# Two memory pairs worked in steps inside two stick-breaking pairs, with output and latent weights in other buffers

## The chip, the cores and the metric

The kernel runs on one core of one Trainium2 chip. The metric is the device time of one execution in microseconds (us). The core has five engines that work on queues of their own: TensorE (PE; its weight loads are shown as PEld), VectorE (DVE), ScalarE (ACT), GpSimd (POOL) and SyncE (SP), which here issues all DMA transfers.

## The reference

Two layers over 2048 tokens of width 1024. Each layer projects the normalized tokens once, and four groups of four heads (64 wide) use the result:

```
h = layer_norm(x); mem_n = layer_norm(mem)              # mem: 256 rows
for l in range(2):
    fq, fk, fv, f, sq, sk, sv, c_q, c_kv, k_rot, mq, gate = split(h @ w_in[l])
    fox: causal softmax(q k / 8 + cum(log_sigmoid(f + b))_q - cum(...)_k) v
    sb : w = sigmoid(z) * prod of (1 - sigmoid(z)) over the later valid keys;  w v   # z = q k / 8
    mla: q, k, v from rms_norm(c_q), rms_norm(c_kv) by two more weights; rope on 32 columns; causal softmax
    mem: softmax(mq mk / 8) mv     # mk, mv = mem_n @ w_mem_kv[l]; all 256 rows, no mask
    y = (concat(fox, sb, mla, mem) * silu(gate)) @ w_out[l]
    h = layer_norm(sqrt(2) * h + y)
```

## The kernel before

**Tiling.** Every factor of a matmul is held as two f16 parts (high and low), and a product is three matmuls (`mm3`, lines 276 to 278). Tokens are worked in 4 chunks of 512. The heads of a group are worked two at a time: a *pair* `fox0` is the first two heads of fox, and so on; eight pairs and one latent step (`lat`: c_q, c_kv, k_rot and the forget column for all tokens) make a layer. `PLAN` (line 45) is their order: lat, fox0, fox1, mla0, mla1, sb0, sb1, and at the end mem0 and mem1 side by side. After them comes the output projection with the layer's normalization (`out_proj`).

**A pair** is a generator (line 707). Its first step loads and splits four weights (`wprep`: load, absolute maximum, a scale by `allmax`, high part on ACT at L146, low part on the DVE at L147). Then each step is a chunk: k, q and v projections, the gate's projection, and attention for two heads. In stick-breaking a work unit is one tile of 128 queries against up to 1024 keys (`stick_tile`): two sigmoids on ACT (L400, L401), the running product from the last key back on the DVE (L403), two multiplications on POOL (L404, L405), the high half on ACT (L411), the low half on the DVE (L412), a transposing DMA (L354), and the matmuls with v (L859). In memory a head of a chunk is eight score matmuls (L803), maxima on the DVE (L807, L808), four Exps on ACT (L811), the halves (L814, L815), a transposing DMA and four matmuls (L820). `half_sum` (L451, L452) adds the two partial outputs; an epilogue (`norm_gate`, `emit_g`) multiplies by the gate and stores to DRAM (`gd`). The epilogue of a chunk is put off (`pending`) until after the next chunk's gate.

**Order and buffers.** The order in which Python issues the steps is a priority: a scheduler at build time walks it and puts each instruction into its engine's queue as soon as its inputs and a buffer are there, so later steps can come early. Buffers are pools of equal places: `sbp` (10 places of 4 KB a partition, `granule`: x, scores, sigmoids, weights of attention, rows of the output), `rawp` (5, loads of weights), `wp` (5, split weights), `qp` (2, queries), `kp` and `vp` (5 each, keys and values), `ptp` (2, transposed weights of attention), `phl` (3, halves on their way to the transposing DMA), `gp` (2, gates), and PSUM pools of 4, 2 and 2 banks.

**The output projection** (line 870) first reads `w_out` for its maxima, then reads it again and splits it into eight tiles `wo`: the first four in `ptp`, the other four in `sbp`. Then, for eight blocks of 256 tokens, it loads the gated rows (`load_gc`, into `kp` and `vp`) and the residual (`yt`), and makes 96 matmuls (L937), the addition (L941) and the normalization. In layer 0 it then transposes the result for layer 1, whose `lat` begins by preparing its own weights: half of them in one `wp` place, half in `kp` and `vp` (lines 498 to 508).

## Time and profile before

| what | value |
|---|---|
| median of 3 runs | 3154.68 us (3153.85 to 3159.28) |
| the profiled execution | 3160.48 us, of which span 3158.5 us |
| PE busy, share of span | 2557.1 us, 81% |
| DVE busy | 2280.7 us, 72% |
| ACT busy | 1913.3 us, 61% |
| POOL busy | 1561.7 us, 49% |

The span is the time from the first to the last instruction; what lies around it is 2 us. Times inside the trace count from the span's start. The shares are means over stages that have different limits, so the rows further down go by stage. A busy PE is not a PE at its peak, because matmuls are pipelined and their ends are modelled: the 512-column matmul is listed with 0.38 us, while in the output projection 791 matmuls end in 170.4 us, 0.22 us each.

### The profile page before, as it was taken

To read this page: it belongs to the slowest core of one execution; us is meant where nothing else is said; L and a number is where in the kernel's file an instruction comes from. 1 tells how busy PE (TensorE), PEld (TensorE's weight loads), DVE (VectorE), ACT (ScalarE), POOL (GpSimd) and SP (SyncE) were. 2 spreads that over 40 slices of the span, in tenths; PEclk is the share of its full clock that TensorE was granted. 3 is DMA by queue.
4 is the path that set the end of the run, shared out by engine and by line. 5 is a ranking of instruction groups with operands and counts; after the bars stand their busy time and mean duration, and the time that the engine had idled before them with its cause. 6 is when DMAs were issued, how large, how long until landed. Compare 5 with 4: busy or idle time off the path is not lost. (4 is left out here: it accounts for less than half of the span.)

```text
span 3158.5 us, 47091 instructions
## 1 busy us (share of the span) xinstructions
PE 2557.1 (81%) x16412; PEld 1374.9 (44%) x16412; DVE 2280.7 (72%) x4377; ACT 1913.3 (61%) x3543; POOL 1561.7 (49%) x1079
## 2 busy tenths in 40 slices
PE   2589897888986784798978899878889768659898
PEld 2345453444553442444434545444445435334443
DVE  7756767867679989757655475577676998994565
ACT  3447667877766676474234566677767766755600
POOL 5305545555678687443210246455657867772400
PEclk9889998999998897799989999999989889769999
DMA  7748978888755745657845478897977475465752
GB/s 190 196 126 167 191 154 188 176 174 174 150 103 115 155 87 112 139 119 191 235 116 126 90 162 163 165 189 157 176 157 135 91 168 101 96 148 114 170 181 100
DMA packets 1225038, 469.46 MB, mean 149 GB/s; under 512 B 1040304, under 2 KB 1184944, under 8 KB 1224656
## 3 DMA queue, kind: packets, MB, share of 16 engines
q1 hardware_dynamic: 1224800, 466.46, 67.8%
q8 instruction: 128, 2.10, 0.3%
q14 instruction: 110, 0.90, 0.1%
HBM read 141.07 MB, written 50.53 MB: 61 GB/s over the span
## 5 line engine op out<-in xcount | busy, mean ns | idle before, releaser
L389 POOL TENSOR_TENSOR hl<-sb,hl 128x1024 f16<-128x1024 f32 (+7 forms) x384 | 609.1, 1599 | 686.3 <-ACT hl L388 503.9
L332 PE MATMUL s<-k,q 128*128 128x512 f16 (+3 forms) x1920 | 529.4, 378 | 117.7 <-ACT sg L401 34.0
L859 PE MATMUL o<-pt,v 128*128 128x256 f16 (+3 forms) x3456 | 429.4, 299 | 200.3 <-DMA pt<-hl 194.8
L405 POOL TENSOR_TENSOR sg<-sg,kp 128x127 f32<-128x127 f32 (+3 forms) x192 | 384.4, 2004 | 119.7 <-DVE kp L403 95.3
L381 ACT ACTIVATE sb<-sb,sm,sc_all 128x1024 f32<-128x1024 f32 (+7 forms) x384 | 376.5, 981 | 76.0 <-DVE sm L377 75.4
L859 PEld LDWEIGHTS <-v 128*64 128x64 f16 (+1 forms) x3456 | 245.0, 112 | 401.7 <-DMA pt<-hl 201.3
L388 ACT CAST hl<-sb 128x1024 f16<-128x1024 f32 (+7 forms) x384 | 297.7, 791 | 184.2 <-DMA pt<-hl 174.0
L937 PE MATMUL s<-wo,gc 128*128 128x512 f16 x1536 | 335.2, 381 | 0.4 <-DVE yt L941 0.4
L332 PEld LDWEIGHTS <-q 128*128 128x128 f16 x1920 | 185.2, 104 | 321.0 <-issue 201.8
L412 DVE TENSOR_TENSOR hl<-sg,hl 128x128 f16<-128x128 f32 (+3 forms) x192 | 241.9, 1267 | 44.0 <-ACT hl L411 43.0
L411 ACT CAST hl<-sg 128x128 f16<-128x128 f32 (+3 forms) x192 | 152.9, 798 | 177.5 <-DMA pt<-hl 104.4
L369 DVE CUSTOM_DVE_ANT_0 sb<-s,fb 128x512 f32<-128x512 f32 (+2 forms) x320 | 184.3, 607 | 102.9 <-DMA fb<-fds 39.6
L371 DVE TENSOR_SCALAR_CACHE_REDUCE sb<-s 128x512 f32<-128x512 f32 (+2 forms) x320 | 185.5, 606 | 72.1 <-POOL hl L389 39.8
L937 PEld LDWEIGHTS <-gc 128*128 128x128 f16 x1536 | 150.9, 98 | 182.2 <-issue 3.9
L401 ACT ACTIVATE sg<-s,sc_all 128x512 f32<-128x512 f32 (+2 forms) x320 | 199.6, 629 | 40.4 <-POOL sg L405 22.1
L403 DVE TENSOR_TENSOR_SCAN kp<-kp 128x384 f32<-128x384 f32 (+7 forms) x128 | 216.6, 1705 | 8.8 <-ACT kp L400 7.7
L400 ACT ACTIVATE kp<-s,sc_all 128x512 f32<-128x512 f32 (+2 forms) x320 | 200.0, 627 | 29.0 <-PE s L332 9.4
L276 PE MATMUL pv<-w,hT 128*128 128x128 f16 x1024 | 191.6, 227 | 24.6 <-DVE k L286 24.6
L456 POOL TENSOR_TENSOR og<-og,sg 128x512 f32<-128x512 f32 x64 | 99.2, 1550 | 223.2 <-DVE og L452 124.0
L276 PE MATMUL pg<-hT,w 128*128 128x512 f16 x512 | 197.0, 385 | 8.1 <-DVE sb L371 3.7
L277 PE MATMUL pg<-hT,w 128*128 128x512 f16 x512 | 196.3, 383 | 0.0
L278 PE MATMUL pg<-hT,w 128*128 128x512 f16 x512 | 195.9, 383 | 0.0
(238 smaller groups left out, 5930.1 us busy)
## 6 DMA issues: line engine op xcount, KB each, us to landing
raw<-in_w_in_dram SPq DMA_DIRECT2D x100, 256.0 KB, 4.7
q<-q SPq DMA_DIRECT2D x128, 128.0 KB, 2.8
fb<-fds SPq DMA_DIRECT2D x32, 512.0 KB, 4.0
gd<-gh SPq DMA_DIRECT2D x128, 128.0 KB, 2.6
raw<-in_w_out_dram SPq DMA_DIRECT2D x64, 256.0 KB, 3.8
gc<-gd SPq DMA_DIRECT2D x64, 256.0 KB, 4.0
yt<-ah SPq DMA_DIRECT2D x32, 512.0 KB, 5.3
raw<-ctd SPq DMA_DIRECT2D x48, 256.0 KB, 3.1
```

The lines of the kernel that those rows point to most:

```text
L276: T.matmul(ps, lh, rh, start=(first and k == 0), stop=False)
L332: T.matmul(ps[:, :m], qs[:, h, v, j * P:(j + 1) * P], ks[c][:, h, :m], start=(v == 0), stop=last)
L381: A.activation(t, t, AF.Exp, scale=sc, bias=sm[:, j, 2:3], accum_out=su[:, b, col + j:col + j + 1])
L388: A.copy(hi, t)
L389: G.tensor_tensor(lo, t, hi, op=ALU.subtract)
L400: A.activation(keep[:, o:o + m], ps[:, :m], AF.Sigmoid, scale=nsc)
L401: A.activation(w[:, o:o + m], ps[:, :m], AF.Sigmoid, scale=sc)
L403: V.tensor_tensor_scan(keep[:, ::-1], keep[:, ::-1], keep[:, ::-1], cy, op0=ALU.mult, op1=ALU.bypass)
L405: G.tensor_tensor(w[:, :n - 1], w[:, :n - 1], keep[:, 1:n], op=ALU.mult)
L412: V.tensor_tensor(lo, w, hi, op=ALU.subtract)
L859: T.matmul(o[r0:r1, oc + j0 * P:oc + 256], vs[k // 4][:, k % 4, h, 0:r1 - r0], pcol(pt, a, k % 8, kb, j0), start=(n == 1), stop=(n == total))
L937: T.matmul(ps, gc[a][k // 4][:, k % 4, t * P:(t + 1) * P], wo[k][:, b2, n * 512:(n + 1) * 512], start=(k == 0 and a == 0 and b2 == 0), sto ...
```

## The change

1. `PLAN` joins mem0 with sb0 and mem1 with sb1. A pair now gives way (`yield`) after the gate, after each memory head, and after each stick-breaking half (two query tiles against up to 1024 keys), so a memory pair has 12 steps behind its first and a stick-breaking pair 28. `TURNS` is the order in which they alternate: ten steps of stick-breaking (chunks 0 and 1), then memory in between in chunks 2 and 3.
2. The epilogue of a memory or stick-breaking chunk runs at once; `og` has two places.
3. Pools: `wp` 5 to 6, `sbp` 10 to 9, `kf` 2 to 1, and most small tiles fewer.
4. The split output weights `wo` lie in `wp` (six) and `qp` (two).
5. The latent weights are a function of their own, `latent_w`, called before the layer: in layer 0 after the start of the input's normalization, in layer 1 in the output projection of layer 0, ahead of its loop. The half that lay in `wp` lies in two `sbp` places.
6. The gated rows of even blocks are loaded into `rawp`, those of odd blocks into `kp` and `vp`.

```diff
-PLAN = [['lat'], ['fox0'], ['fox1'], ['mla0'], ['mla1'], ['sb0'], ['sb1'], ['mem0', 'mem1']]
+PLAN = [['lat'], ['fox0'], ['fox1'], ['mla0'], ['mla1'], ['mem0', 'sb0'], ['mem1', 'sb1']]
+TURNS = {'mem': [1] * 10 + [1, 1, 1, 0] + [1, 1, 0] * 3 + [1] + [1, 0] * 8}
-    wp = pool("wp", 5)
+    wp = pool("wp", 6)
-    sbp = pool("sbp", 10)
+    sbp = pool("sbp", 9)
...
+    def latent_w(l, s_h, u_h):
+        W = w_in[l]
+        at, sc_at[0] = sc_at[0], NSC - 32
...
                         if k % 4 == 0:
-                            w4 = wp.tile([P, 4, 512], F16, name=nm("w"), tag="w")
+                        w4 = granule("w4", (P, 4, 512), F16)
...
-    def layer(l, hT, s_h, u_h, ah):
+    def layer(l, hT, s_h, u_h, ah, latw, norm):
...
         def latent():
-            gqk = raw_tile()[:, :384]
...
+            gqk, lops, uu, u_f = info["latw"]
             yield
             for c in range(NCH):
-                kf = op.tile([P, 4, 36], F32, name=nm("kf"), tag="kf", bufs=2)
+                kf = op.tile([P, 4, 36], F32, name=nm("kf"), tag="kf", bufs=1)
...
                     sg = gate_tanh(wg, u2, c, hops(c))
+                yield
                 flush()
-                og = op.tile([P, 512], F32, name=nm("og"), tag="og")
+                og = op.tile([P, 512], F32, name=nm("og"), tag="og", bufs=2)
...
                         half_sum(o, og, h)
+                        yield
                         continue
...
-                    half_sum(o, og, h)
+                            if (g, b) == (2 * c + 1, bs[-1]):
+                                half_sum(o, og, h)
+                            yield
                 def epilogue(c=c, og=og, sg=sg, su=su):
...
                 pending.append(epilogue)
-                yield
+                if kind in ("mem", "sb"):
+                    flush()
...
-                if k < 4:
-                    if k % 2 == 0:
-                        w2 = ptp.tile([P, 2, 2, D], F16, name=nm("wo"), tag="pt")
-                    w = w2[:, k % 2]
+                if k < 6:
+                    w = wp.tile([P, 2, D], F16, name=nm("wo"), tag="w")
                 else:
-                    w = granule("wo", (P, 2, D), F16)
+                    w = qp.tile([P, 2, D], F16, name=nm("wo"), tag="q")
...
-                info["out"] = (hTn, s_n, u_n, ahn)
+                info["out"] = (hTn, s_n, u_n, ahn, latent_w(l + 1, s_n, u_n))
...
-                        t = (kp, vp)[u].tile([P, 4, 256], F16, name=nm("gc"), tag="kv"[u])
+                        if c2 % 2:
+                            t = (kp, vp)[u].tile([P, 4, 256], F16, name=nm("gc"), tag="kv"[u])
+                        else:
+                            t = raw_tile().bitcast(F16).rearrange("p (k t) -> p k t", k=4)
...
-            for c in range(NCH):
-                if norm:
+            if norm:
+                for _ in range(NCH):
                     next(norm, None)
-                if c == AHEAD[gi] and gi + 1 < len(PLAN):
-                    coming = start(gi + 1)
-                for g in gens:
-                    next(g)
+                    next(gens[0])
+            turns = TURNS.get(PLAN[gi][0][:-1])
+            for g in turns or []:
+                next(gens[g], None)
+            for g in gens:
+                for _ in g:
+                    pass
...
     for l in range(DEPTH):
         sc_at[0] = 32
-        r = layer(l, hT, s_h, u_h, ah)
+        norm = input_norm() if l == 0 else None
+        if norm:
+            next(norm)
+            latw = latent_w(l, s_h, u_h)
+        r = layer(l, hT, s_h, u_h, ah, latw, norm)
```

## Rows read from the trace of the kernel before

**Rows 1.** Windows by stage; the header names the columns.
```profile
core 0: us, PE busy (x) PEld busy (x) DVE busy (x) ACT busy (x) POOL busy (x), PEclk, DMA share, GB/s
795.00:935.00 140.00, 128.19 (x975) 74.20 (x974) 96.00 (x172) 101.80 (x176) 93.13 (x73) 0.98 0.71 135
935.00:1058.00 123.00, 86.38 (x573) 46.85 (x572) 119.21 (x128) 86.29 (x148) 96.62 (x60) 0.82 0.63 131
1058.00:1320.00 262.00, 179.82 (x1212) 99.41 (x1211) 234.63 (x239) 160.47 (x278) 185.46 (x116) 0.82 0.59 118
1200.00:1300.00 100.00, 47.78 (x235) 22.90 (x234) 95.72 (x100) 60.75 (x99) 76.25 (x38) 0.68 0.62 129
1320.00:1444.00 124.00, 113.42 (x619) 57.48 (x618) 75.42 (x144) 87.62 (x205) 47.22 (x34) 0.95 0.56 124
795.00:1444.00 649.00, 507.82 (x3375) 277.94 (x3374) 525.26 (x681) 436.18 (x805) 422.43 (x281) 0.88 0.62 125
1444.00:1618.00 174.00, 170.36 (x791) 76.96 (x789) 112.09 (x198) 47.91 (x67) 40.64 (x24) 1.00 0.74 200
1636.00:1707.00 71.00, 71.00 (x397) 39.04 (x396) 25.05 (x97) 30.18 (x112) 0.00 (x0) 0.98 0.41 97
2331.00:2985.00 654.00, 519.13 (x3399) 283.12 (x3400) 524.37 (x685) 440.77 (x816) 423.50 (x284) 0.87 0.61 126
```

**Rows 2.** Lines of the DVE in 795:1444: count | busy us, mean ns | idle before, releaser.
```profile
L412 DVE TENSOR_TENSOR hl<-sg,hl 128x1024 f16<-128x1024 f32 (+4 forms) x96 | 121.7, 1274 | 24.1 <-ACT hl L411 23.5
L403 DVE TENSOR_TENSOR_SCAN kp<-kp 128x128 f32<-128x128 f32 (+3 forms) x64 | 108.6, 1711 | 4.0 <-ACT kp L400 3.5
L403 DVE TENSOR_TENSOR_SCAN kp<-kp,cy 128x1024 f32<-128x1024 f32 x32 | 76.4, 2389 | 0.6 <-ACT kp L400 0.5
...
L452 DVE TENSOR_TENSOR og<-o,og 64x512 f32<-64x512 f32 x32 | 22.0, 686 | 15.5 <-ACT og L451 15.1
L807 DVE TENSOR_REDUCE smm<-s 128x2 f32<-128x512 f32 x32 | 21.4, 686 | 14.6 <-PE s L803 14.5
```

**Rows 3.** Timeline of ACT, 1330:1345: start us, us, engine, line, operation.
```profile
1333.31 0.69 ACT L430 ACTIVATE sg<-pg,sc_all 128x512 f32<-128x512 f32 x1 [2.27 <-PE pg L278]
1335.26 0.59 ACT L285 ACTIVATE q<-pq 64x512 f16<-64x512 f32 x1 [1.27 <-PE pq L278]
1335.87 1.28 ACT L811 ACT_TABLE_LOAD   x1
1337.17 0.56 ACT L811 ACTIVATE pe<-s,smm,sc_all 128x256 f32<-128x256 f32 x1
```

**Rows 4.** Lines of ACT, whole trace: the table loads at L421 and L811.
```profile
L421 ACT ACT_TABLE_LOAD x2 | 2.6, 1283 | 0.0
L811 ACT ACT_TABLE_LOAD x2 | 2.6, 1283 | 0.0
```

**Rows 5.** Timeline of PE, 1610:1640, between projection and latent stage of layer 1.
```profile
1609.76 4.70 PE L937 MATMUL s<-wo,gc 128*128 128x512 f16 x21
...
1632.05 0.27 PE L137 MATMUL pm<-id_bf,am 128*2 128x128 bf16 x1 [15.69 <-DVE am L135]
...
1635.33 1.56 PE L276 MATMUL pl<-w,hT 128*128 128x420 f16 x4 [2.23 <-ACT w L146]
```

**Rows 6.** Timeline of SP, 60:120: issues of x loads.
```profile
81.36 2.46 SPq L1018 DMA_DIRECT2D xt<-in_x_dram  x4
...
109.73 0.59 SPq L1018 DMA_DIRECT2D xt<-in_x_dram  x1
```

**Rows 7.** Waits of PE, 98:162: us in total, times, longest us.
```profile
PE pl L276 <- DMA hT<-hl: 21.2, 1, 21.2
```

**Rows 8.** Waits of the DVE, 240:795.
```profile
DVE sb L371 <- POOL hl L389: 18.8, 13, 4.9
...
DVE sb L369 <- POOL hl L389: 9.2, 5, 5.3
```

**Rows 9.** Source line 165, load of memory weights: ns min/median/max, first and last us.
```profile
L165 SPq DMA_DIRECT2D raw<-in_w_mem_kv_dram x16: 368/448/1091, 1051.6 to 2816.9; - x16
```

More of the change, by code (lines that the diff above doesn't have):

```diff
@@ L112, in sc_tile @@
         sc_at[0] += n
-        assert sc_at[0] <= NSC
+        assert sc_at[0] <= (NSC - 32 if sc_at[0] - n < NSC - 32 else NSC)
         return sc_all[:, sc_at[0] - n:sc_at[0]]
@@ L199, in bound_gb @@
     def bound_gb(g, b, f):
-        m = smp.tile([P, 8], F32, name=nm("gb"), tag="gb", bufs=4)
+        m = smp.tile([P, 8], F32, name=nm("gb"), tag="gb", bufs=2)
         absmax(m[:, 0:1], g)
@@ L211, in rsqrt @@
     def rsqrt(v, n, pool=False):
-        y = smp.tile([P, 8], F32, name=nm("ry"), tag="ry", bufs=4)[:, :n]
-        t = smp.tile([P, 8], F32, name=nm("rt"), tag="rt", bufs=4)[:, :n]
+        y = smp.tile([P, 8], F32, name=nm("ry"), tag="ry", bufs=2)[:, :n]
+        t = smp.tile([P, 8], F32, name=nm("rt"), tag="rt", bufs=2)[:, :n]
         A.activation(y, v, AF.Sqrt)
@@ L462, in emit_g, with S_of, lat_w @@
             dma(dst[:, :, u * 256:(u + 1) * 256], gh)
-    def layer(l, hT, s_h, u_h, ah):
+    def S_of(s, u, s_x, u_x):
+        S_, U_ = sc_tile(), sc_tile()
+        V.tensor_scalar(S_, s, s_x, E20, op0=ALU.mult, op1=ALU.mult)
+        V.tensor_scalar(U_, u, u_x, 2.0 ** 20, op0=ALU.mult, op1=ALU.mult)
+        return S_, U_
+    def latent_w(l, s_h, u_h):
+        W = w_in[l]
+        at, sc_at[0] = sc_at[0], NSC - 32
+        gqk = raw_tile()[:, :384]
+        dma(gqk[:, 0:256], mla_q_norm_g[l].partition_broadcast(P))
+        dma(gqk[:, 256:384], mla_kv_norm_g[l].partition_broadcast(P))
+        s_cq, u_cq = bound_gb(gqk[:, 0:256], None, 16.0)
+        s_ck, u_ck = bound_gb(gqk[:, 256:384], None, 16.0)
+        V.tensor_scalar(gqk[:, 0:256], gqk[:, 0:256], s_cq, None, op0=ALU.mult)
+        V.tensor_scalar(gqk[:, 256:384], gqk[:, 256:384], s_ck, None, op0=ALU.mult)
+        wl = {}
+        for k in range(0, KC, 2):
+            for a in range(2):
+                if k < 4:
+                    if k % 4 == 0:
+                        w4 = granule("w4", (P, 4, 512), F16)
+                        for i in range(0, 4, 2):
+                            wl[k + i, a] = w4[:, i:i + 2, :420]
+                else:
+                    w2 = (kp, vp)[a].tile([P, 2, 512], F16, name=nm("w"), tag="kv"[a])
+                    wl[k, a] = w2[:, :, :420]
+        def lat_w(o):
+            return lambda j, a, b: [wl[k, a][:, :, o + j * P:o + (j + 1) * P] for k in range(4 * b, 4 * b + 4, 2)]
+        (_, s1, u1), = wprep([([W[:, C_CQ:C_CQ + P], W[:, C_CQ + P:C_CQ + 2 * P]], lat_w(0))])
+        rawt = raw_tile()[:, :288].rearrange("p (k n) -> p k n", n=36)
+        dma(rawt[:, :, 0:32], W[:, C_KR:C_KR + 32].rearrange("(k p) n -> p k n", p=P))
+        dma(rawt[:, :, 32:36], W[:, C_F:C_F + 4].rearrange("(k p) n -> p k n", p=P))
+        (_, s3, u3), (s4, u4) = wprep([([W[:, C_CQ + 2 * P:C_CQ + 3 * P]], lat_w(256))],
+                                      lambda b: absmax(b, rawt.rearrange("p k n -> p (k n)")))
+        for k in range(0, KC, 2):
+            split(wl[k, 0][:, :, 384:420], wl[k, 1][:, :, 384:420], rawt[:, k:k + 2], s4)
+        lops = [tuple(wl[k - k % 2, a][:, k % 2] for a in range(2)) for k in range(KC)]
+        uu = sc_tile(2)
+        V.tensor_scalar(uu[:, 0:1], u1, u_h, None, op0=ALU.mult)
+        V.tensor_scalar(uu[:, 1:2], u3, u_h, None, op0=ALU.mult)
+        S_kr, U_kr = S_of(s4, u4, s_h, u_h)
+        u_f = sc_tile()
+        V.tensor_scalar(u_f, u4, u_h, None, op0=ALU.mult)
+        assert sc_at[0] <= NSC
+        sc_at[0] = at
+        return (s_cq, u_cq, s_ck, u_ck, S_kr, U_kr), (gqk, lops, uu, u_f)
@@ L474, in layer @@
         info = {}
+        info["lat"], info["latw"] = latw
         def hops(c, kcs=range(KC)):
@@ L921, in load_gc @@
                     for u in range(2):
-                        t = (kp, vp)[u].tile([P, 4, 256], F16, name=nm("gc"), tag="kv"[u])
+                        if c2 % 2:
+                            t = (kp, vp)[u].tile([P, 4, 256], F16, name=nm("gc"), tag="kv"[u])
+                        else:
+                            t = raw_tile().bitcast(F16).rearrange("p (k t) -> p k t", k=4)
                         dma(t, gd[u * 4:u * 4 + 4, :, a, c2 * 256:(c2 + 1) * 256].rearrange("k p t -> p k t"))
@@ L966, in start @@
             return gens
-        norm = input_norm() if l == 0 else None
-        if norm:
-            next(norm)
         coming = start(0)
```

57 lines of the change are left out of this document (8 added, 49 removed).

## Prediction

> **What bounds the kernel now.** I read the windows by stage first, then the DVE's instructions by line in the stretch that the change rebuilds, then the ACT timeline at a change of function, and last the waits at the places where a buffer goes or a transfer is moved.
>
> The windows [rows 1] cut layer 0. The four-head softmax stages end near 795 us; both stick-breaking pairs run until 1320, the two memory pairs until 1444, the output projection until 1618, and layer 1 repeats this (its stick-breaking and memory pairs lie at 2331 to 2985). From 795 to 1444 no engine is full: DVE 525.3 of 649 us, PE 507.8, ACT 436.2, POOL 422.4. But the parts differ. In 795:935, where the early chunks' projections are made, PE is full (128.2 of 140) and DVE is not (96.0). In 935:1058, which is mostly later chunks, DVE is full (119.2 of 123) while PE has 86.4. In 1200:1300, the last chunk of the second pair, DVE has 95.7 of 100, PE 47.8, and the granted clock fell to 0.68. In the memory stage it turns round: PE 113.4 of 124, DVE 75.4. So two stages with opposite limits stand one behind the other. The lines of the DVE [rows 2] say what fills it: the running product (L403) 108.6 + 76.4 us, the low half of the weights (L412) 121.7 us; memory adds its maxima (L807) 21.4 us.
>
> The output projection is PE alone (170.4 of 174 us), and after it comes a hole of some 20 us in which PE does almost nothing [rows 5].
>
> **The change part by part.** *Memory inside stick-breaking.* Nothing is computed less; the question is how full the DVE gets. The stretch holds 525.3 us of DVE work in layer 0 and 524.4 in layer 1. The fullest whole stage with a beginning and an end in it, 1058:1320, keeps the DVE 234.6/262 = 0.896 busy. At that share 525.3 us take 586 us. The ends to either side are the mean of now (0.81: 649 us, no gain) and the share of 935:1058 (0.97: 542 us). I take 0.896, because the new stage also has begin and end, and its first ten steps (chunks 0 and 1) have no memory step in them, so 795:935 keeps its 44 us of idle DVE.
>
> To that comes ACT's function tables. The rows around 1333 [rows 3] show the tanh gate run on the table that stick-breaking left, but the first Exp of memory (L811) waits for a table load: the ACT ends at 1335.85, the load takes 1.28 us, and the Exp starts at 1337.17; so 1.3 us a change. Now there is one such change each way per layer [rows 4]. With memory heads between stick-breaking steps, each of the 16 memory heads by chunk in a layer (2 pairs, 4 chunks, 2 heads) is at least one trip to Exp and back: 32 loads, 42 us of ACT a layer. If the two score groups of a head are parted by sigmoids it is 64 loads, 83 us; if each of the 64 Exps stands alone, 128 loads, 166 us. From below, zero (heads bunched together). I take 32 to 64; then ACT holds 478 to 519 us, which at 0.896 is 533 to 579, still under the DVE's 586. So most loads hide behind the DVE; a quarter of the least sum, 10 us a layer, is charged. The Trainium skill (ScalarE: Activation LUTs, "Table sets: the hidden batching unit") says to do all activations of one table set before those of another, which speaks against this change, and under "What ACT_TABLE_LOAD costs" it counts about 2.66 us a switch with a drain; the row above shows no drain beside the load, and by that figure the 32 loads would be an estimated 85 us a layer.
>
> *The new tail.* Today the memory stage covers the end of stick-breaking (1200 to 1320), and the projection is dense from 1444 on [rows 1]. After, the end of stick-breaking is the end of the stage. Six of eight output weights go where projection weights lie, free before the end; two go where the queries lie, free only after the last scores. And in layer 0 the latent weights stand ahead of the projection in the order, with loads through the five raw places and with key and value places that the last attention holds. The nearest row for such a stall is the 15.7 us that PE waited, until 1632, for a weight's scale [rows 5]. Bounds 0 and 16 us more than now; I take 10. A stage then takes 586.3 + 20 = 606.3 us in layer 0, 42.7 less than 649, and 524.4/0.896 + 20 = 605.3 in layer 1, 48.7 less than 654: 91 us saved.
>
> *Latent weights ahead.* The hole is plain in the PE timeline [rows 5]: projection ends at 1614.4, PE waits 15.7 us for the scale and 2.2 us for the split weights, and the latent matmuls begin at 1635.3. With the weights made before, the first three chunks of layer 1 are ready to go at 1614; the hole goes, 15.7 + 2.2 = 18 us, once (layer 0 has no earlier projection). Next late is the last chunk's normalization and transposing, which three of four chunks of latent matmuls cover (71 us for all four, 1636:1707 [rows 1]); without that cover it would be about the same 18 us again, so 0 is the other bound.
>
> *Smaller places.* The general work buffers go from 10 to 9, and the latent weights take two of them. In the input stage, 8 were free for x and latent rows and 5 will be. The four x loads of chunk 2 were issued only at 81.4 and the first of chunk 3 at 109.7 [rows 6], when places came free, and PE waited 21.2 us for a chunk's transposed input [rows 7]. A load that misses its turn waits at most for the next places, 109.7 - 81.4 = 28 us; so the cost lies between 0 and 28, and I take 12. In the softmax stages the DVE waited 18.8 + 9.2 us in layer 0, 240:795, for the POOL's low half [rows 8], the instruction that gives a buffer back; with one buffer in ten gone the cost lies between 0 and those 28 us a layer; such a wait costs only where nothing else keeps the chain going, and I take 5 a layer, 10 in all. The sixth weight place can bring the next pair's weights earlier; I take nothing, and at most the 15.7 us of [rows 5] at a change of pair. Each of two streams now has one set of queries in place of two; memory's matmuls and the DVE's backlog cover that, at nothing, and without that cover its nearest size is the 15.1 us for which the DVE waited at the half sums [rows 2]. The rest (flush at once, two output tiles, fewer small tiles) moves the order of single operations whose engines, POOL and ACT, are 0.65 and 0.67 busy in the stretch [rows 1]: nothing; if they did wait, the same 15.1 us is the size.
>
> Sum against the profiled execution, 3160.5 us (span 3158.5): -91 - 18 + 12 + 10 = -87. The median of the runs is 3154.7, 5.8 below the profiled one; I subtract from the median: **3068**.
>
> **The rivals.** *The projection comes forward too* (0.16). In 1200:1300 PE stands idle 52 us. If six output weights are split in that tail and the early columns' gated rows, long written, are loaded, projection matmuls fill it. For it: the order is eager, since the first load of memory weights was issued at 1051.6 [rows 9], 270 us ahead of their stage. Against: DVE must split those weights while full. At 35 of the 52 us a layer: 3068 - 70 = 2998.
>
> *Little comes of it* (0.20). Memory's steps lie in chunks 2 and 3 alone, where DVE is 0.97 full; each memory us of DVE adds a us there. Then only the memory stage's slack goes, 124 - 75.4 = 49 us, less 20 for loads and tail: 29 a layer, 58, with -18 + 22 from the rest: 3155 - 54 = 3101.
>
> *The table loads stand on the path* (slower, 0.16). ACT takes its work in order, and sigmoid, high half and low half of a stick-breaking step go from ACT to DVE to POOL and back, so a load ahead of a sigmoid can hold the DVE up by its whole 1.3 us. The stage without loads is 586 + 10 us; 53 us are left to 649, so from 41 loads on the path in a layer it is longer than now. At 64, 83 us: 679 us in layer 0 and 678 in layer 1, 30 and 24 longer, with +4 from the rest: 3155 + 58 = 3213; near the point itself it is 3159. If all 128 were needed, ACT alone would hold 436 + 166 = 602 us and be the bound. For it: 64 Exps a layer in pairs, each pair behind its own maxima. Against: ACT has 213 us of 649 free now, so a load often finds it idle. The Trainium skill's rule on table sets (same page and section) names this outcome; 4 of these loads in the trace of before are too few to show it.
>
> *No change in sum* (0.06): the merging brings 58 as in the second rival and the latent weights 18, while the input stage takes its bound, 28, and the buffers 24 of their 28 us a layer: 58 + 18 - 28 - 48 = 0, so 3155. Within 0.2%, 6 us, is about what a measurement can tell from no change.
>
> **How the numbers follow.** The forecast, 3068, has 0.42. Faster: 0.42 + 0.16 + 0.20 = 0.78; same 0.06; slower 0.16. The forecast's own range is 3038 to 3104 (DVE share 0.92 to 0.87 in both layers, 571 to 604 us in place of 586). Cutting the far end of the first rival and the half of the slower one that lies above 3175 leaves out under 0.2: 2990 to 3175.
>
> **What would show it.** The stretch that was 795 to 1444 should be near 606 us, DVE 0.88 busy, with no stretch like 1320:1444. ACT_TABLE_LOAD should count 64 to 130 over the program; many more, with the DVE waiting for ACT behind them, is the slower rival. Latent matmuls of layer 1 should follow the projection with under 5 us between. PE's wait for the transposed input should not grow by more than 12 us. It is wrong if the DVE in the merged stage stays under 0.83 busy, if PE idles over 25 us ahead of the projection, or if the softmax stages stretch by over 15 us a layer.

## The result and the profile after

The changed kernel takes 3308.6 us (median of 4 runs, 3301.38 to 3311.99), the kernel before 3154.26 us (4 runs) beside it: ratio 1.0477, 95% interval 1.0459 to 1.0494. It is 4.8% slower, where I forecast 3068 us, 2.7% faster, and it lies above the range (2990 to 3175). The profiled execution has a span of 3310.2 us, 151.7 longer than before.

The windows of the changed kernel, cut at its own stages, answer to [rows 1].

```profile
core 0: us, PE busy (x) PEld busy (x) DVE busy (x) ACT busy (x) POOL busy (x), PEclk, DMA share, GB/s
833.00:913.00 80.00, 66.80 (x472) 37.76 (x470) 45.26 (x88) 37.69 (x68) 29.20 (x19) 0.91 0.81 186
913.00:983.00 70.00, 62.25 (x475) 35.78 (x472) 53.19 (x47) 42.13 (x81) 41.22 (x35) 0.98 0.36 66
983.00:1175.00 192.00, 130.49 (x707) 64.44 (x708) 152.30 (x204) 135.19 (x240) 104.46 (x72) 0.78 0.52 102
1175.00:1241.00 66.00, 48.24 (x351) 28.35 (x350) 39.75 (x42) 34.44 (x62) 32.62 (x19) 0.83 0.53 111
...
1311.00:1485.00 174.00, 109.98 (x614) 55.45 (x612) 134.23 (x142) 134.16 (x239) 105.78 (x73) 0.77 0.55 111
1485.00:1553.00 68.00, 24.49 (x100) 10.85 (x99) 47.01 (x81) 24.58 (x45) 29.21 (x16) 0.56 0.67 168
833.00:1553.00 720.00, 503.74 (x3194) 268.12 (x3192) 524.36 (x649) 451.31 (x815) 385.38 (x270) 0.82 0.55 114
1553.00:1714.00 161.00, 161.00 (x748) 73.00 (x747) 90.53 (x149) 32.14 (x35) 30.55 (x14) 1.00 0.63 164
2461.00:3138.00 677.00, 491.94 (x3166) 266.02 (x3167) 479.56 (x579) 446.61 (x794) 369.30 (x263) 0.84 0.53 111
```

The work is the same over the whole program: the DVE is busy 2270.0 us, 2280.7 before. The stretches above begin at the last masked score of the softmax stages, those of [rows 1] some 50 us ahead of it. Cut like the changed kernel, the kernel before has

```profile
847.00:1451.00 604.00, 464.61 (x3034) 252.35 (x3032) 490.27 (x576) 403.12 (x756) 398.35 (x263) 0.87 0.60 123
2386.00:2986.00 600.00, 467.85 (x3034) 254.59 (x3033) 487.48 (x576) 403.06 (x754) 394.29 (x263) 0.87 0.60 124
```

So the DVE went from 0.81 busy in both layers to 0.73 (524.4 of 720 us) and 0.71 (479.6 of 677); the prediction had 0.896. That 524.4 us lies so near the 525.3 of [rows 1] comes from the two cuts. Two kinds of rows are new. Where the pairs change (833:913, 1175:1241) the DVE has 45 of 80 and 40 of 66 us. And where memory runs between stick-breaking steps (983:1175, 1311:1485) nothing is full: the DVE has 0.79 and 0.77, PE 0.68 and 0.63, ACT 0.70 and 0.77.

The next table cuts both layers of each kernel by matmuls of the traces: the last masked score of the softmax stages, the first and the last masked score of each stick-breaking pair, and the 25th matmul of the output projection, from which it runs without gaps. The cuts are at whole microseconds. "Change-over" is the time ahead of a pair's first masked score, "group" from its first to its last, "tail" from the last to the projection. In the kernel before, the tail holds the memory stage.

| kernel, layer | change-over 1 | group 1 | change-over 2 | group 2 | tail | sum |
|---|---|---|---|---|---|---|
| before, 0 | 10 | 199 | 16 | 199 | 180 | 604 |
| after, 0 | 80 | 262 | 66 | 244 | 68 | 720 |
| before, 1 | 11 | 196 | 16 | 201 | 176 | 600 |
| after, 1 | 50 | 270 | 62 | 264 | 31 | 677 |

The tails fell by 257 us in all, which is the memory stage gone; the groups grew by 245 and the change-overs by 205. That is +193. The first softmax score of layer 0 comes at 182.4 us and not at 196.7 (-14), and from the last matmul of layer 0's projection to the first softmax score of layer 1 it is 106 us and not 129 (-23). The softmax stages lose 1 us in sum (651 and 640 us against 650 and 642), the projections 3. 193 - 14 - 23 - 1 - 3 gives the 152 us of the span.

The timeline of ACT around one memory head inside a stick-breaking chunk answers to [rows 3].

```profile
1002.21 1.28 ACT L822 ACT_TABLE_LOAD   x1
1003.51 0.56 ACT L822 ACTIVATE pe<-s,smm,sc_all 128x256 f32<-128x256 f32 x1
...
1004.61 1.04 ACT L412 CAST hl<-sg 128x1024 f16<-128x1024 f32 x1
1005.54 0.57 ACT L822 ACTIVATE pe<-s,smm,sc_all 128x256 f32<-128x256 f32 x1
...
1006.78 1.04 ACT L825 CAST hl<-pe 128x1024 f16<-128x1024 f32 x1
1007.84 1.28 ACT L401 ACT_TABLE_LOAD   x1
1009.14 0.58 ACT L401 ACTIVATE kp<-s,sc_all 128x384 f32<-128x384 f32 x1
```

The timelines of PE and of the DVE in the same stretch:

```profile
1004.76 1.01 PE L333 MATMUL s<-k,q 128*128 128x512 f16 x2 [6.69 <-ACT pe L822]
1005.57 0.63 PE L277 MATMUL pq<-hT,w 128*128 128x512 f16 x1
...
1009.67 0.38 PE L278 MATMUL pq<-hT,w 128*128 128x512 f16 x1
```

```profile
1005.68 1.23 DVE L413 TENSOR_TENSOR hl<-sg,hl 128x1024 f16<-128x1024 f32 x1 [1.82 <-ACT hl L412]
1009.75 1.09 DVE L404 TENSOR_TENSOR_SCAN kp<-kp 128x384 f32<-128x384 f32 x1 [2.85 <-ACT kp L401]
```

One head takes ACT from 1002.21 to 1009.14 without a sigmoid. The stick-breaking scores (L333) that start at 1004.76 have waited 6.69 us, from before the head's first Exp, for a score bank that the Exps still read, and the DVE's running product waits 2.85 us for the first sigmoid behind the head. The waits of 913:1485 in all:

```profile
PE o L871 <- DMA pt<-hl: 62.2, 25, 7.9
ACT hl L412 <- POOL sg L406: 60.7, 39, 4.3
...
DVE kp L404 <- ACT kp L401: 35.3, 21, 4.1
PE s L333 <- ACT pe L822: 33.7, 12, 7.7
DVE hl L413 <- ACT hl L412: 27.9, 23, 3.6
```

Lines of the DVE in 833:1553, which answer to [rows 2]:

```profile
L413 DVE TENSOR_TENSOR hl<-sg,hl 128x1024 f16<-128x1024 f32 (+4 forms) x96 | 126.9, 1326 | 28.6 <-ACT hl L412 27.9
L404 DVE TENSOR_TENSOR_SCAN kp<-kp 128x128 f32<-128x128 f32 (+3 forms) x64 | 101.0, 1590 | 21.7 <-ACT kp L401 21.0
L404 DVE TENSOR_TENSOR_SCAN kp<-kp,cy 128x1024 f32<-128x1024 f32 x32 | 83.7, 2624 | 14.3 <-ACT kp L401 14.2
```

The DVE waited 4.6 us ahead of its running products before [rows 2]; now it is 36.0. The table loads of ACT, whole trace (70 in all; 15 before), beside [rows 4]:

```profile
L822 ACT ACT_TABLE_LOAD x29 | 37.2, 1283 | 15.5 <-DVE smm L819 12.4 <-DVE cy L409 2.7
L401 ACT ACT_TABLE_LOAD x27 | 34.6, 1283 | 0.4
```

And the timeline of PE between projection and latent stage, against the hole of [rows 5]:

```profile
1704.74 9.23 PE L953 MATMUL s<-wo,gc 128*128 128x512 f16 x42
1713.81 0.34 PE L277 MATMUL pl<-w,hT 128*128 128x420 f16 x1
```

The latent matmuls follow at once.

### The profile page after: what moved, and what is told of

Same layout as the page of the kernel before. It is cut to its first block, busy times and chain, and to the rows that moved or that the text cites. A ratio compares the mean times of both kernels' runs of the same rounds, so it can differ in the third digit from the quotient of the medians.

```text
span 3310.2 us, 47080 instructions
## 1 busy us (share of the span) xinstructions
PE 2599.8 (79%) x16412; PEld 1383.6 (42%) x16412; DVE 2270.0 (69%) x4377; ACT 1981.4 (60%) x3598; POOL 1513.7 (46%) x1079
## 5 line engine op out<-in xcount | busy, mean ns | idle before, releaser
L333 PE MATMUL s<-k,q 128*128 128x512 f16 (+3 forms) x1920 | 537.6, 379 | 202.8 <-ACT pe L822 67.9
L406 POOL TENSOR_TENSOR sg<-sg,kp 128x127 f32<-128x127 f32 (+3 forms) x192 | 349.0, 1818 | 55.6 <-DVE kp L404 39.1
L333 PEld LDWEIGHTS <-q 128*128 128x128 f16 x1920 | 185.7, 104 | 378.0 <-issue 254.7
L404 DVE TENSOR_TENSOR_SCAN kp<-kp 128x384 f32<-128x384 f32 (+7 forms) x128 | 205.7, 1619 | 44.5 <-ACT kp L401 43.3
L401 ACT ACTIVATE kp<-s,sc_all 128x512 f32<-128x512 f32 (+2 forms) x320 | 202.8, 634 | 18.9 <-PE s L337 9.5
L277 PE MATMUL pg<-hT,w 128*128 128x512 f16 x512 | 201.6, 394 | 7.0 <-DVE sb L372 4.3
L278 PE MATMUL pg<-hT,w 128*128 128x512 f16 x512 | 200.4, 391 | 0.0
L279 PE MATMUL pg<-hT,w 128*128 128x512 f16 x512 | 199.6, 390 | 0.0
L278 PEld LDWEIGHTS <-w 128*128 128x128 f16 x1264 | 127.9, 101 | 163.8 <-issue 44.9
L277 PEld LDWEIGHTS <-w 128*128 128x128 f16 x1264 | 128.4, 102 | 155.1 <-issue 20.6
```

Source lines behind the costliest of these rows:

```text
L277: T.matmul(ps, lh, rh, start=(first and k == 0), stop=False)
L278: T.matmul(ps, lh, rl, start=False, stop=False)
L333: T.matmul(ps[:, :m], qs[:, h, v, j * P:(j + 1) * P], ks[c][:, h, :m], start=(v == 0), stop=last)
L401: A.activation(keep[:, o:o + m], ps[:, :m], AF.Sigmoid, scale=nsc)
L404: V.tensor_tensor_scan(keep[:, ::-1], keep[:, ::-1], keep[:, ::-1], cy, op0=ALU.mult, op1=ALU.bypass)
L406: G.tensor_tensor(w[:, :n - 1], w[:, :n - 1], keep[:, 1:n], op=ALU.mult)
```

## The experiments

Each edit is to the changed kernel if nothing else is said. Ratios are to the kernel before.

**The joining or the rest of the change?** `unmerged` takes back the joining alone.

```diff
-PLAN = [..., ['mem0', 'sb0'], ['mem1', 'sb1']]
+PLAN = [..., ['sb0'], ['sb1'], ['mem0', 'mem1']]
-TURNS = {'mem': [1] * 10 + [1, 1, 1, 0] + [1, 1, 0] * 3 + [1] + [1, 0] * 8}
+TURNS = {'mem': [0, 0, 0, 1, 1, 1] * 4}
```

> The changed kernel with the old order of pairs (both stick-breaking pairs alone, the two memory pairs side by side at the end), everything else as changed. If the merging costs the time, whatever its mechanism, this runs at 3120 to 3170 us, the latent hole of 18 us saved and small losses from 9 work buffers. If the other parts (latent weights ahead, output weights in other places, fewer buffers) cost it, it stays over 3270 us.

3184.6 us, 1.0093 (1.0078 to 1.0108): near the range of the first theory (3120 to 3170), 15 us above it. Its stretches are 656 and 616 us, so joining costs 720 - 656 = 64 and 677 - 616 = 61 us, and the rest of the change costs 52 + 16 us in them against before. Its change-overs are 10, 18, 10 and 32 us with the same pools as the changed kernel, so the smaller pools alone do not make those of 50 to 80. The first key projection of `sb0` starts at 786.8 us here, 42 us ahead of the last softmax score; in the changed kernel the first projection of a new pair starts at 844.8, 12 us behind that score. Of the 52 us, 44 lie in the tail of layer 0 (223.5 us, 179.6 before); the tail of layer 1, with no latent weights in it, is 181 (176 before). Waits of PE in the tail of layer 0, 1262:1490:

```profile
PE s L953 <- DMA raw<-gd: 15.1, 2, 11.4
...
```

The projection has begun (1463.8) and waits 11.4 us for gated rows, which now come into the raw places through which the latent weights go too. So, by the difference of the two tails, the latent weights cost about 39 us ahead of the projection (44 in the layer that has them, 5 in the other) and give 23 behind it.

**Table loads.** `sigmoid_for_exp` puts Sigmoid in place of memory's Exp (another function), so nothing is switched. `sigmoid_no_max` also leaves out the row maxima.

```diff
-    A.activation(pe[:, j], psv[:, j % 2], AF.Exp, scale=sc, bias=sm[:, 4 + j:5 + j], ...
+    A.activation(pe[:, j], psv[:, j % 2], AF.Sigmoid, scale=sc, bias=sm[:, 4 + j:5 + j], ...
```

> The changed kernel with Sigmoid in place of Exp in the memory heads alone (the weights of memory attention are then other numbers), so that the order of all instructions is the same and the 56 table loads of the merged stages are gone. Loads on the path: 56 x 1.3 = 73 us or more, 3215 to 3240 us. Loads hidden (places and latency set the time): less than 25 us, 3285 to 3308 us.

> After with Sigmoid in place of the memory's Exp, so no table is switched, and without the memory's row maxima and the step that makes biases of them (the bias is another tile that is there early). Leaves out the softmax's maxima, and its Exp is another function. To be compared with the run that only has Sigmoid for Exp, 3289 us. Theory A, the chain score, maximum, bias, Exp holds two score banks and the DVE's queue while the stick-breaking halves wait: 60 to 100 us less, 3190 to 3230. Theory B, the memory head costs by the sum of its work on PE and ACT in queues of fixed order, and the maxima are only some 2 us of DVE time per head: under 25 us less, 3265 to 3290.

The first: 13 loads in place of 70 and 3289.3 us, 1.0429 (1.0409 to 1.0448): 19 us for 57 loads of 1.28 us (by the two ratios 15 us, with some 8 to either side), so about three quarters of their 73 us were hidden. The second: 3243.9 us, 1.0288 (1.0273 to 1.0304), a further 45 us. It lies between the two theories. The DVE work left out is some 72 us in the two layers (L818 21.3 and L819 14.8 in the stretch of layer 0), so the 45 are less than that work itself; a chain that multiplied it is not seen.

**Which places?** The change took buffers away, and two streams share them. Each of these gives more places of one kind or two; room comes from `sbp`, so `sbp8` and the pools alone are told too.

```diff
-    sbp = pool("sbp", 9)
+    sbp = pool("sbp", 8)      # sbp8; with kp, vp 6: sbp8_kv6; with qp 3: sbp8_qp3
+    sbp = pool("sbp", 7)      # kp, vp 6 and qp 3: sbp7_kv6_qp3; rawp 9: sbp7_raw9; wp 8: sbp7_wp8
+    sbp = pool("sbp", 6)      # kp, vp 6 and rawp 9: kv6_raw9
```

> The changed kernel with 8 work buffers in place of 9. If the number of stick-breaking units in flight is what holds the DVE at 0.78 inside the merged stages, one place less costs 60 us or more (over 3370 us). If the change-over of pairs is what costs, it costs under 25 us (under 3335 us).

> The changed kernel with 8 work buffers and 6 places each for keys and values in place of 5. Against the run with 8 work buffers alone: if key and value places hold the second pair's start, the 66 and 62 us from the last score of the first merged stage to the first of the second shrink to under 40 us, and the time falls by 40 us or more. If weights, queries or work buffers hold it, under 15 us.

> The changed kernel with 8 work buffers and three query places in place of two, to be read against the run with 8 work buffers alone (3392 us). If the single query place of each stream holds the next chunk or the change-over, the time falls by 40 us or more and chunks 2 and 3 shorten; if not, by under 10 us.

> The changed kernel with 7 work buffers, 6 places each for keys and values and three for queries. The softmax stages will be longer for want of work buffers, so the change-overs are read alone. If finished queries and keys that wait for a place hold the two PSUM banks of the projections, and so the next weights' scales, all three change-overs that follow a joined stage fall from 62 to 72 us to under 35. If it is the eight weights in six places or their loads, they stay over 50.

> After with nine raw weight places in place of five; room for them comes from seven stick-breaking buffers in place of nine, which by the runs with eight and seven costs the softmax stages some 35 to 60 us each and the joined groups little. Theory A, the four weight groups of a joined start go one by one through five raw places (a group holds four) and that makes the change-over: the change-overs, 79, 63, 51 and 61 us with seven buffers, fall by 20 to 30 us each. Theory B, the weights wait for something else (the prepared places, or the queue of the engine that scales them): the change-overs stay within 8 us of those numbers. The whole time is not what is read here; it should lie near 3450 to 3500 us by either.

> After with more places for prepared weights (eight) and seven stick-breaking buffers. Theory A, the last weight group waits for a prepared place that the memory of the pair before gives up late (in the trace of after its scale matmul comes some 75 us behind the third one's): the change-overs of 79, 63, 51 and 61 us fall by 20 to 30 us. Theory B, the place is not what it waits for, or the work behind it takes the wait over: they stay within 8 us. Whole time near 3450 to 3500 us by either unless A holds, then 80 to 100 us less.

> After with nine raw places and six key and value places each, with six stick-breaking buffers in place of nine to make room (the softmax stages grow again by that). Theory A, several kinds of places hold the next pair back in turn, and each alone only moved the wait: with both kinds the change-overs (57, 74, 42, 60 us with nine raw places alone; 79, 63, 51, 61 with six key and value places alone) fall to 35 us or less at the second pairs. Theory B, the projections of the next pair stand behind the last attention of the pair before in PE's queue, and two streams have two sets of them to do before the first score: they stay above 50 us.

| run | us, ratio (interval) | change-overs 0, 0, 1, 1 | groups |
|---|---|---|---|
| after | 3308.6, 1.0477 (1.0459 to 1.0494) | 80, 66, 50, 62 | 262, 244, 270, 264 |
| sbp8 | 3391.9, 1.0750 (1.0733 to 1.0766) | 84, 72, 53, 65 | 252, 249, 273, 255 |
| sbp8_kv6 | 3372.6, 1.0688 (1.0672 to 1.0704) | 80, 70, 54, 63 | 252, 243, 269, 266 |
| sbp8_qp3 | 3336.1, 1.0556 (1.0521 to 1.0591) | 80, 62, 53, 61 | 246, 243, 265, 260 |
| sbp7_kv6_qp3 | 3493.2, 1.1069 (1.1045 to 1.1092) | 79, 63, 51, 61 | 257, 251, 262, 260 |
| sbp7_raw9 | 3485.7, 1.1049 (1.1027 to 1.1071) | 57, 74, 42, 60 | 248, 249, 261, 254 |
| sbp7_wp8 | 3518.9, 1.1154 (1.1133 to 1.1174) | 55, 65, 30, 58 | 262, 243, 268, 262 |
| kv6_raw9 | 3521.2, 1.1157 (1.1136 to 1.1177) | 57, 67, 35, 59 | 246, 241, 269, 257 |

The whole times rise because the softmax stages need the work buffers: 651 and 640 us with nine, 685 and 674 with eight, 709 and 704 with seven (in `sbp7_kv6_qp3`). So the 3392 us of `sbp8` lie in the range of its first theory, but not by that theory: inside the joined groups fewer buffers cost nothing. A third query place does give something: against `sbp8` the joined stretches of `sbp8_qp3` are 34 and 7 us shorter (694 and 668 us in place of 728 and 675), and the softmax stage of layer 1 is 23 us shorter. But its change-overs stay at 53 to 80 us. The first change-over falls with raw or weight places, but the softmax stage ahead of it grows (softmax and change-over 1 of layer 0 together: 789 us in `sbp7_kv6_qp3`, 792 in `sbp7_raw9`, 808 in `sbp7_wp8`; of layer 1: 754, 750, 747). The second, where stage and change-over don't trade like this, stays at 58 to 74 us in every run. So the theory that places of a kind make the change-overs is not borne out, one by one or raw with key and value places together.

What the second change-over consists of shows where the weights are early, in `sbp7_raw9` (its four scales are made by 1238 us, 64 us ahead of the last score). Windows of its change-over, 1302 to 1376 us:

```profile
1302.00:1325.00 23.00, 8.99 (x44) 4.68 (x43) 22.88 (x13) 14.28 (x23) 18.77 (x10) 0.58 0.52 108
1325.00:1376.00 51.00, 43.98 (x331) 28.19 (x330) 22.40 (x32) 21.86 (x45) 14.66 (x11) 0.89 0.54 109
```

First the old pair's last weights keep the DVE full (22.88 of 23 us) while PE has 8.99 us of work; then PE makes the projections of the new chunk for two streams (43.98 of 51 us) while the DVE has little. In the kernel before, keys, queries and values of the next pair were projected inside the last chunk of the pair before, where PE had room, and 16 us were left. Lines of PE in 1002:1056, one of the three matmuls of each product, and then in the second change-over of the changed kernel, 1175:1241:

```profile
L276 PE MATMUL pv<-w,hT 128*128 128x128 f16 x30 | 6.5, 247 | 3.8 <-DVE k L286 3.8
L276 PE MATMUL pq<-hT,w 128*128 128x512 f16 x8 | 3.5, 443 | 0.0
L276 PE MATMUL pk<-hT,w 128*128 128x512 f16 x8 | 3.0, 380 | 0.0
```

```profile
L277 PE MATMUL pg<-hT,w 128*128 128x512 f16 x24 | 10.2, 423 | 0.0
...
L277 PE MATMUL pv<-w,hT 128*128 128x128 f16 x32 | 5.5, 219 | 0.0
```

In the changed kernel two sets of queries and the keys of `sb1` come ahead of the last score too (1143 to 1167 us). Behind it stand memory's keys and values, three gates, a third set of queries and the values of `sb1`; in layer 1 the keys, queries and values of `sb1` all stand behind it. What PE meets first at this joined start of layer 0 is the rows of `mem`. Their load and PE's wait for it:

```profile
L756 SPq DMA_DIRECT2D memT<-memTd x2: 359/468/577, 1184.0 to 1188.6; - x2
...
  DMA memT<-memTd: 9.0, 1
```

The last score of the pair before was at 1175 us. These rows lie in two `sbp` places, which stick-breaking uses too, and their load came 9 to 20 us after the last score of pair 0 of layer 0 in each run of the table (37 to 41 in layer 1); the other projections of 1175:1241 stood behind that matmul in PE's queue. They are not all of it: in layer 1 keys and queries of `sb1` were projected at 2791 to 2807 us, ahead of the rows' matmul at 2826, and that change-over is 62 us as well. Whether another place for these rows would let the projections forward was not tried.

**Order.** `sb_first` starts stick-breaking ahead of memory, `sb_high` gives its halves a higher priority, `mem_behind` does all 28 stick-breaking steps before the 12 of memory.

```diff
-PLAN = [..., ['mem0', 'sb0'], ['mem1', 'sb1']]
+PLAN = [..., ['sb0', 'mem0'], ['sb1', 'mem1']]                             # sb_first, turns exchanged
+    with tc.high_priority(offset=300 if kind == "sb" else 0):               # sb_high, around the halves
+TURNS = {'mem': [1] * 28 + [0] * 12}                                       # mem_behind
```

> The changed kernel with the order of the two starts turned: the four stick-breaking weights are prepared ahead of the four memory weights, the steps then alternate as before. If the change-over (80, 66, 50 and 62 us from the last score of one stage to the first stick-breaking score) is the wait of stick-breaking's weights behind memory's in six places, each shrinks to 15 to 40 us and the time falls by 60 us or more. If queries, keys and values or gates hold it, under 20 us.

> The changed kernel with the stick-breaking halves given a higher place in the build's order (300 instructions ahead), so that a memory step goes into an engine's queue only where no stick-breaking instruction is ready. If a memory head costs its 6 us because it is put ahead of the next sigmoids, chunks 2 and 3 (90 and 102 us) come to 65 to 80 us and the whole to under 3240 us. If it costs because the two streams share places and banks, whoever goes first, the whole stays within 25 us of 3309.

> The changed kernel with all 28 stick-breaking steps ahead of the 12 memory steps in each joined stage. If steps in turns are what costs, chunks 2 and 3 go back to some 60 and 70 us, memory's heads follow at the end of each stage and are partly hidden behind the next start: 3200 to 3240 us. If the change-over costs most, it grows with the memory steps at the end, and the whole is at or over 3300.

| run | us, ratio (interval) | change-overs | groups | tails |
|---|---|---|---|---|
| sb_first | 3279.9, 1.0375 (1.0348 to 1.0401) | 49, 97, 58, 56 | 231, 221, 263, 257 | 103, 29 |
| sb_high | 3271.7, 1.0367 (1.0350 to 1.0384) | 73, 64, 53, 59 | 252, 249, 260, 251 | 65, 31 |
| mem_behind | 3273.0, 1.0371 (1.0343 to 1.0400) | 78, 141, 49, 132 | 193, 193, 183, 177 | 112, 102 |

Each is about 1% better than the changed kernel and none is near the kernel before; all three lie outside the ranges of both of their theories. With `sb_first` the first change-over falls from 80 to 49 us, but the four together are as long as without it (260 and 258 us): the second, 97 us, now holds four memory heads of the first pair. `mem_behind` says most: with no memory head inside, a group takes 177 to 193 us, no more than before the change; the heads then stand behind it, in change-over and tail, and the stretches are 717 and 643 us against 720 and 677. Whether heads stand between the stick-breaking steps or behind them makes 3 and 34 us of difference, the wrong way round for an overlap.

**The heads themselves.** `mem_no_heads` leaves out memory's attention (scores to half sums, and the division by the sums; the gate, scaled down, stands for its output) and keeps weights and projections. `mem_scores_p` takes its score banks from the projections' PSUM pool, so stick-breaking keeps its four.

```diff
+    if kind == "mem":                                              # mem_no_heads
+        yield
+        continue
-    pss = [s_tile() for _ in range(2)]                            # mem_scores_p
+    pss = [ps_p.tile([P, 512], F32, name=nm("s"), tag="p") for _ in range(2)]
```

> The changed kernel with the attention of the memory heads left out (scores, maxima, Exps, halves, transposes, products with v and the normalization by the sum); its projections, gates and epilogues stay. If heads that share ACT, DVE and PSUM with stick-breaking make chunks 2 and 3 long, these go back to about 60 and 70 us, 130 us less in all, near 3180. If it is the projections of memory and the places that its queries and gates hold, the chunks stay over 80 us.

> The changed kernel with the two score banks of a memory head taken from the PSUM pool of the projections (two banks) in place of the four banks that stick-breaking's scores use. If the units stand still because memory's scores hold two of the four banks until their Exps, chunks 2 and 3 of a merged stage (90 and 102 us in the first) come down to 75 and 85, some 100 us in all: 3200 to 3230. If the banks don't matter, within 15 us of 3309.

Without the heads: 3113.5 us, 0.9852 (0.9818 to 0.9885), 195 us less for 32 heads, 6.1 each. Windows of its layer 0:

```profile
898.00:1099.00 201.00, 151.66 (x1017) 81.24 (x1016) 172.37 (x168) 136.83 (x245) 139.08 (x103) 0.89 0.48 94
1099.00:1173.00 74.00, 59.92 (x410) 32.82 (x409) 49.16 (x77) 27.79 (x46) 25.07 (x18) 0.88 0.51 118
...
827.00:1442.00 615.00, 449.36 (x2971) 241.24 (x2970) 478.46 (x553) 355.86 (x627) 352.61 (x254) 0.85 0.56 119
```

The groups are 201, 206, 223 and 210 us (196 to 201 in the kernel before), but the change-overs are 71, 74, 52 and 63 us without any head in the kernel. The stretch of layer 0 is 615 us: with nothing left of memory but weights, projections and gate, longer than the 604 of the kernel before with all of it. In layer 1, whose tail has no latent weights, it is 574 against 600. With the scores in the projections' banks: 3380.0 us, 1.0694 (1.0664 to 1.0724), outside both theories. The groups lose 26 us in all, the change-overs (85, 96, 55, 86) gain 64: two banks that the projections need are worse to share than four.

**The two small parts by themselves, in the kernel before.** `before_latents_ahead` prepares layer 1's latent weights inside the output projection at its seventh block of eight, `before_latents_c2` at its third. `before_w4_granule` changes one line, which is in the change too.

```diff
+    if c2 == 6 and not last:                                       # before_latents_c2: c2 == 2
+        info["out"] += (latent_w(l + 1, s_n, u_n),)
-    w4 = wp.tile([P, 4, 512], F16, name=nm("w"), tag="w")         # before_w4_granule
+    w4 = granule("w4", (P, 4, 512), F16)
```

> The kernel before with one part of the change alone: the latent weights of layer 1 made inside the output projection of layer 0, ahead of its seventh block of eight. If the hole of 18 us between projection and latent stage can be had without the rest, 3125 to 3140 us against 3155 of before, with no stall ahead of the projection. If the weights' loads and places hold the projection up in turn, 3150 to 3165.

> The kernel before with the latent weights prepared early in the output projection (at its third column group, not its seventh). With them at the seventh the time stayed 3153 us: the latents followed at once, but the projection was 13 us longer by waits of PE for the scale matmul. Theory A, the scale is late there only because it was asked for too late or too close to its inputs: at the third group the wait goes, the projection is 163 us again and the hole of some 20 us is gone, 3125 to 3145. Theory B, PE meets a scale matmul whose input the DVE has not made yet wherever it stands in its queue, and the wait only moves: within 6 us of 3153.

> The kernel before with one line of the change: the first half of the latent weights lies in two work buffers and no longer in two of the five places of projection weights. Theory A, these two places made the first pair's weights late, in both layers or in layer 0 alone: the first score of layer 0 comes at about 182 us in place of 197, and the whole time is 3135 to 3145. Theory B, the 15 us come from another part of the change (the order of the input stage, the sixth weight place): 3150 to 3160, first score at 197.

Latents ahead: 3152.8 us, 0.9991 (0.9979 to 1.0003). Third block: 3152.5 us, 0.9990 (0.9980 to 0.9999). In both the latent matmuls follow at once, but the projection takes 176 and 196 us for 164. Waits of PE in the projection of `before_latents_c2`:

```profile
PE s L948 <- DMA gc<-gd: 16.0, 3, 12.1
PE pm L142 <- DVE ad L141: 1.6, 1, 1.6
```

The wait that theory B named, for the scale, is nearly gone here; another came, for gated rows. Half of the latent weights lie in the key and value places into which these rows are loaded; that this makes the wait is argued, not tried. Of the 32 us more, 19 are waits and 7 are projections of the next pair, drawn forward: most of the hole moved into the projection.

The one line: 3141.5 us, 0.9951 (0.9938 to 0.9965), the only version with the full work that is faster than both kernels by more than 0.2%. In the kernel before, the half of the latent weights that it moves fills two of the five weight places, not one. The first score comes at 181 us. Timelines of PE at the start, first the kernel before, then this one:

```profile
38.13 0.16 PE L142 MATMUL pm<-ad,ones_bf 1*128 1x1 bf16 x1 [6.96 <-DVE ad L141]
49.30 0.58 PE L276 MATMUL pl<-w,hT 128*128 128x256 f16 x2 [11.01 <-ACT w L146]
```

```profile
28.10 0.16 PE L142 MATMUL pm<-ad,ones_bf 1*128 1x1 bf16 x1 [0.61 <-DVE ad L141]
34.27 0.40 PE L276 MATMUL pl<-w,hT 128*128 128x256 f16 x1 [6.01 <-DMA hT<-hl]
```

The first latent matmuls start at 34.3 us, not at 49.3, and wait for the normalized input, no longer for their weights. The changed kernel has 182 and 34.3.

## Why the prediction was wrong

**The step that failed** is "At that share 525.3 us take 586 us". It took a busy share from a stage in which one stream ran and the next pair's projections filled PE's gaps, and gave it to a stage in which two streams start, run and end together. With its two additions it made the stages 43 and 49 us shorter; from the last softmax score to the projection they are 116 and 77 us longer. The DVE's work is nearly the same, but its share fell from 0.81 to 0.73 and 0.71 in the two layers where it was to rise to 0.896. So the upper bound of that step, "0.81: 649 us, no gain", was no bound. Two things make the difference. The start of a joined pair has two sets of projections ahead of its first score, and they come forward into the stage before only in part or not at all, where one stream's did nearly whole (+205 us in four change-overs; these stay with the heads left out, and most of them goes with the joining taken back). And the heads find no room inside the chunks: the chunks without memory steps stay at 29 to 42 us, those with them go from 56 to 70 us to 84 to 109, 32 heads cost 195 us, and putting the heads behind the stick-breaking steps does not lengthen the stages (717 and 643 us). Of the 6.1 us of a head, some 0.6 is its table loads (19 us in 32), 1.4 its maxima (45 in 32); what the other four are split into (score banks, ACT's queue, work) was not told apart.

The sign to look for had a slip of its own: 525.3 us in 606 are a share of 0.87, not 0.88.

**Table loads.** Their number is right: 70 over the program, forecast 64 to 130; 56 of them at L822 and L401, 28 a layer, a little under the 32 to 64 that were taken. That they hide is right too: 10 us a layer were charged, 19 us in all are shown. The rival "table loads stand on the path" ended on the right side and for the wrong reason: its price was 83 us a layer. The Trainium skill (ScalarE: Activation LUTs, "What ACT_TABLE_LOAD costs") counts 2.66 us a switch; by it the 57 loads would be an estimated 152 us. No run here shows that: a load is 1.28 us in the trace, and taking 57 away gave 19.

**The rival "little comes of it"** held that the DVE's work adds up in chunks 2 and 3, because it is full there. That memory's steps add up is right, but the DVE is not full there (0.79, 0.77). The rows of one head show waits between engines in its place; how much of the delay they make was not measured.

**The tail.** It was put at 10 us more for the projection's start, 16 at the most. From the last score to the dense projection it is 31 us in layer 1 and 68 in layer 0, and PE is idle for 12 and 44 of them; over 25 was a sign of being wrong. The rows of [rows 1] had hidden a tail of this kind behind the memory stage. In layer 0 the last matmuls with v wait 25.4 us for the transposing DMA (longest 11.8), and the projection 17.1 us for gated rows.

**Latent weights ahead.** The hole went, as forecast (18 us; 23 shown). Its price, part of the 10 us for the tail, was too small: `unmerged` pays some 39 us ahead of the projection, and both versions of the kernel before paid the gain back inside it.

**One set of queries for each stream** was put at nothing ("memory's matmuls and the DVE's backlog cover that"). By `sbp8_qp3` against `sbp8`, a third query place is worth some 40 us in the two joined stretches.

**Smaller places.** "I take 12" for the input stage had the wrong sign. It looked at x loads alone and not at the latent weights' own wait, 6.96 and 11.01 us in the timeline at 30 to 50 us. PE's wait for a transposed chunk in this part [rows 7] went from 21.2 us to 0.9. The row of PE in the changed kernel, 90:162:

```profile
PE pl L277 <- DMA hT<-hl: 0.9, 1, 0.9
```

The softmax stages were charged 10 us for one buffer less. Against the kernel before they show none, and the DVE's waits for POOL's low half are those of [rows 8]:

```profile
DVE sb L372 <- POOL hl L390: 17.4, 12, 5.0
...
DVE sb L370 <- POOL hl L390: 10.2, 6, 3.2
```

But `before_w4_granule`, with ten buffers and the same place for the latent weights, has stages of 635 and 636 us, 16 and 4 less than the changed kernel; so the tenth buffer may have a price that this line's gain covers. From nine to eight it is 35 and 34 us.

**What stays open.** What keeps the joined starts' projections from coming forward: the load of `mem`'s rows into `sbp` places stands at the head of PE's queue in layer 0, but that it is the cause was not tried, and in layer 1 it is not the first thing that PE meets; nor were all three kinds of places (raw, key and value, queries) together, for which there was no room.

## What to carry to other kernels

A busy share belongs to the order that produced it: before joining two stages, ask what the start of the joined stage has to do before its first useful step, and in what gap that was done until now. Two streams that share engines' queues and a few banks can add up, as here; the trial that shows it cheaply is to put one stream wholly behind the other and compare the sums. Work moved ahead of a stage to close a hole behind it can take that stage's own places, so look at what the stage loads through them first.

## What the runs showed that I had not expected

The step from nine work buffers to eight costs some 35 us in each of the softmax stages (`sbp8`) and nothing in the joined groups. The two buffers that hold the first latent weights decide 15 us at the start of the program. And this wait of PE cost more than its length: ahead of it the granted clock was 1.00, and behind the 6.69 us at 1004.76 the projections ran at half the clock, by the windows

```profile
1005.60:1009.40 3.80, 3.80 (x10) 1.34 (x9) 1.23 (x1) 3.74 (x8) 1.50 (x1) 0.50 0.71 147
1009.70:1012.00 2.30, 2.30 (x12) 1.05 (x11) 2.21 (x3) 2.30 (x6) 1.94 (x3) 1.00 0.79 151
```

at the level of 1.2 GHz for ten matmuls, which the timeline shows 0.43 us apart, and at 2.4 GHz after, 0.22 us apart; so about 2 us were added.
